# Differential attention in front of a mixture of experts: scores in three single PSUM banks, transposes in two, a later place for each projected tile's transposes, and the output norm spread over the last turns

## The chip, the core and the metric

The kernel runs on one core of a Trainium2 chip. The metric is the device time of one execution in microseconds (us). Of the kernel before there are three runs, from 1671.71 to 1674.43, median 1672.71, and one more execution that was recorded by the hardware profiler.

## The reference, cut to what matters

Two layers work on 256 latent and 256 context tokens of width 1024. Layer 0 is a short gated convolution and a dense SwiGLU. Layer 1, in which the change lies, is differential attention and a mixture of experts. Its attention has 16 heads of 64 in 8 pairs; only the latent tokens ask, and all 512 tokens answer:

```python
def diff_core(q, k, v, lam):
    logits = einsum('bqhd,bkhd->bhqk', q, k) * (HEAD_DIM ** -0.5)
    p = softmax(logits, axis=-1).reshape(b_, h2 // 2, 2, nq, nk)
    w = p[:, :, 0] - lam * p[:, :, 1]
    return einsum('bhqk,bkhe->bqhe', w, v)          # one value of 128 for each pair

q_l, k_l, v_l = proj(a_lat)     # rms_norm of q and k in each head, then rope_2d
q_c, k_c, v_c = proj(a_ctx)     # rms_norm alone
o = rms_norm(o, sub_g) * (1 - lam_init)             # the output norm, over each 128
h = h + g1 * (o.reshape(..., -1) @ w_out)
...
xs = a_pad[slot_tok]            # top 2 of 8 experts for each token
ys = (silu(xs @ w1) * (xs @ w3)) @ w2               # 2816 hidden
```

## The kernel before, in words

**Products.** A large product is three matmuls in a reduced float type (`mm3`, lines 173 to 176): weight and activation are each split in a high and a low part, and high by high, high by low and low by high are added in PSUM. Weights come from HBM in units of 128x2048 float32 (1 MB), 300 and more of them, one after the other on SP's queue (`loads`). `Parts.pump` (line 72) takes a unit that has landed when a slot is free, writes its high part with a cast (ACT, line 80; DVE, line 78, for the units listed in `HV`, here 0 and 63), and subtracts on DVE for the low part (line 84). Its instructions stand in ACT's and DVE's queues at the place where the program calls `pump`, which is inside `parts.unit` (take the next unit), `release` and `give` (line 119: hand back n spent units and prepare one more).

**Order.** The program has a schedule by hand: each engine executes its instructions in the order in which the Python code issues them. The order around the change is therefore made by calls, and by generators that are advanced a few steps at a time.

**Projections.** Four passes, each for two pairs of heads, project queries, keys and values. A pass gives tiles of 128 tokens by 512 columns: A and B (latent queries and keys), D (context keys), C and E (values). `normed` (line 714) takes A, B and D: ACT squares the tile, DVE multiplies by the rope factors and sums the squares, `seed` (704) makes a first guess of the inverse root on DVE, `newton` (706) refines it in eight small POOL instructions, DVE multiplies (743) and PE transposes the tile in four 128x128 pieces (749) that ACT copies to `qk`. Between these come `yield`s, five behind the Newton steps and three behind the multiplication, and at each PE gets another few products of a projection in between (for one step of `projections`, line 765, three matmuls of 512 columns with A and B, six of 256 with C, D and E).

**Turns.** Sixteen turns, one for each pair of a head and 128 queries, and two more to drain (line 929). Turn m issues, in this order: `turn(m-2)`, PE's four transposes of the weights (843) and ACT's copy `wT` (845); `scores(m)`, two matmuls of 512 columns (815); `top(m)`, the row maxima on DVE (819); `weigh(m-1)`, the difference of the two softmaxes on DVE (836 to 838); `soft(m)`, two exponentials on ACT (828); five steps of `fill`, the projections of passes 1 to 3; the output steps; and `value(m-2)` (851). From turn 11 on no projections are left. There the output norm is worked in: `subnorm` (the inverse root), `scaled` (873), `sub_t` (878 transposes; 879 the high part `onh` on ACT; 880 the low part `onl` on DVE) and `outp`, the output projection, whose weights are units 61 to 64.

**PSUM.** Eight banks. In the turns the pool `pss` has two tiles of two banks each for scores, `psw` one bank for transposes (`wt`), `pso` one for values and `psf` two for projections.

**What follows.** `gated` adds to the residual, the routing ranks the experts, and a gather by one-hot matmuls (1130) brings the tokens of an expert together: its result is evicted by DVE (1134), cast by ACT (1136) and subtracted by DVE (1124). Eight experts of 11 chunks each follow: `up`, the gate (Silu on ACT, 1168, and a product on DVE, 1169), two transposes (1175) and `down`. Units 67 and 68 are the weights of the first chunks.

Of the kernel before, what the change touches and what calls it, by code (L numbers as in the profile page):

```python
# [11 lines left out]
F32 = mybir.dt.float32  # L12
# [8 lines left out]
P = 128  # L21
# [9 lines left out]
GROUPS = (6, 8, 8)  # L31
ADA_PE = (0, 1, 3)
NE = 8
HV = (0, 63)
NCH = FT // 2
LAM = 0.8 - 0.6 * math.exp(-0.3)

# [93 lines left out]
def backbone(ctx: ExitStack, tc: tile.TileContext, i, out):  # L131
# [582 lines left out]
    def normed(n, kind, ps, new):  # L714

        sq = pq.tile([P, T2], F32, name="qsq", bufs=2)
        A.activation(sq, ps, AF.Square)
        x = pq.tile([P, T2], F32, name="qx", bufs=3)
        if kind == "D":
            V.tensor_tensor(out=heads(x), in0=heads(ps), in1=qkg[:, None, 64:].to_broadcast([P, 8, 64]), op=OP.mult)  # L720
        else:
            t = "AB".index(kind)
            z = pq.tile([P, T2], F32, name="qz")
            for a in range(2):
                xs = ps[:, half(a)].rearrange("p (h r b j) -> p h r b j", h=4, r=2, b=2)
# [12 lines left out]
        newton(r, m, e)  # L738
        if kind != "D":
            V.tensor_tensor(out=x, in0=x, in1=z, op=OP.add)  # L740
        for _ in range(5):
            yield
        V.tensor_tensor(out=heads(x), in0=heads(x), in1=r[:, :, None].to_broadcast([P, 8, 64]), op=OP.mult)
        for _ in range(3):
            yield
        pt = new()
        for j in range(4):
            c = j % 2 * 2 + j // 2 if kind == "D" else j
            PE.transpose(pt[:, j * P:(j + 1) * P], x[:, c * P:(c + 1) * P], ident)
        if kind == "D":  # L750
            A.copy(qk[n % 2][:, 2:, T:], pt.rearrange("p (j t) -> p j t", j=2))
        else:
            A.copy(qk[n % 2][:, :, t * P:(t + 1) * P], pt.rearrange("p (j t) -> p j t", j=4))
# [42 lines left out]
    loads.advance()  # L796
    l0.close()

    pss = att.enter_context(tc.tile_pool(name="pss", bufs=2, space=PSUM, reuse_waits="tile"))
    psw = att.enter_context(tc.tile_pool(name="psw", bufs=1, space=PSUM, reuse_waits="tile"))  # L800
    pso = att.enter_context(tc.tile_pool(name="pso", bufs=1, space=PSUM, reuse_waits="tile"))
    psf = att.enter_context(tc.tile_pool(name="psf", bufs=2, space=PSUM, reuse_waits="tile"))
    aw = att.enter_context(tc.tile_pool(name="aw", bufs=1, side="right", reuse_waits="tile"))
# [5 lines left out]
    def scores(m):  # L809
        h, t = heads16[m]  # L810
        n, j = h // 2 % 2, h % 2
        ps = S[m] = pss.tile([P, 2, T2], F32, name="sc")
        for a in range(2):
            r = slice(64 * a, 64 * a + 64)
            PE.matmul(ps[:, a], qk[n][r, j, t * P:(t + 1) * P], qk[n][r, 2 + j], start=True, stop=True)

    def top(m):
        mx = sm.tile([P, 2], F32, name="mx")
        V.tensor_reduce(mx, S[m], axis=AX.X, op=OP.max)
        V.tensor_scalar(mx, mx, -0.125, None, op0=OP.mult)  # L820
        return mx

    def soft(m, mx):
        h, t = heads16[m]
        e = E[m] = aw.tile([P, 2, T2], F32, name="e", bufs=3)
        z1 = sm.tile([P, 1], F32, name="z1")
        for a in range(2):
            A.activation(e[:, a], S[m][:, a], AF.Exp, bias=mx[:, a:a + 1], scale=0.125,
                         accum_out=z1 if a else z0[:, t, h:h + 1])
        return z1  # L830

# [91 lines left out]
    def pull(n):  # L923
        for _ in range(n):
            next(fill, None)
# [3 lines left out]
    for m in range(18):  # L929
        if m > 1:  # L930
            turn(m - 2)
        if m < 16:
            scores(m)
            mx = top(m)
        if 0 <= m - 1 < 16:
            weigh(m - 1, zs.pop(m - 1))
        if m < 16:
            zs[m] = soft(m, mx)
        pull(5)
        if m == 13:  # L940
            subnorm(0, 4, 6)
            outp(ops, LO, (0, 1))
        if m == 14:
            subnorm(1, 4, 6)
            outp(ops, LO, (2, 3))
        if m == 15:
            out1 = pss.tile([P, 2, T2], F32, name="sc")
            ops += [out1[:, a, half(b)] for a in range(2) for b in range(2)]
            outp(ops, HI, (0, 1))
        if m == 16:  # L950
            outp(ops, HI, (2, 3))
        if m == 17:
            scaled(0, 6, 8)
            outp(ops, LO, (4, 5))
        if m > 1:
            value(m - 2)
        pull(5 if m < 11 else 99)
        if m == 10:
            for t in range(2):
                subnorm(t, 0, 4)  # L960
        if m == 11:
            for t in range(2):
                scaled(t, 0, 4)
            proj.close()
            held.close()
            pm = more.enter_context(tc.tile_pool(name="more", bufs=1, reuse_waits="tile"))
            parts.free.extend(part_slots(pm, 1, "x"))
            parts.last_use, xlo = parts.free[-1]
            parts.holding = True
            nh, nl = ([pm.tile([P, D], F32R, name=n), parts.last_use[:, c * D:(c + 1) * D]] for c, n in enumerate(("nh", "nl")))  # L970
            small = routing(pm)
            oh = [pm.tile([P, 2, P], F32R, name=f"oh{t}") for t in range(2)]
            po = att.enter_context(tc.tile_pool(name="on", bufs=1, reuse_waits="tile"))
            onh, onl = (po.tile([P, 8, 2, P], F32R, name=f"on{n}") for n in range(2))
            wo = [parts.unit() for _ in range(2)]
            ops = [psf.tile([P, T2], F32, name="mm") for _ in range(2)]
            ops = [ops[a][:, half(b)] for a in range(2) for b in range(2)]
        if m == 12:
            sub_t(0, 0, 4)
            sub_t(1, 0, 4)  # L980
            parts.pump(1)
        if m == 13:
            wo += [parts.unit() for _ in range(2)]
        if m == 14:
            scaled(0, 4, 6)
            sub_t(0, 4, 6)
        if m == 15:
            scaled(1, 4, 6)
            sub_t(1, 4, 6)
        if m == 16:  # L990
            subnorm(0, 6, 8)
            parts.give(1)

        loads.free.extend({11: ada_slots[:1], 15: ada_slots[1:], 17: later[:1]}.get(m, []))
        loads.advance()
    subnorm(1, 6, 8)
    sub_t(0, 6, 8)
    scaled(1, 6, 8)
    outp(ops, HI, (4, 5))
    sub_t(1, 6, 8)  # L1000
    parts.give(1)

    r = small

# [10 lines left out]
    def route_n():  # L1015

        V.tensor_tensor(out=r["ms"], in0=r["ms2"][:, :, 0], in1=r["ms2"][:, :, 1], op=OP.add)
        A.activation(r["ms"], r["ms"], AF.Sqrt, bias=eps, scale=1.0 / D)
        V.reciprocal(r["ms"], r["ms"])

    def route_h(t, n):

# [41 lines left out]
    for k in range(0, KT, 2):  # L1064
        outp(ops, [k, k + 1], (6, 7))
        for n in range(k, k + 2):
            gated(ops[n], n, mod1[8 + k // 2], 0)
        if k == 4:
            both = pss.tile([P, 2, T2], F32, name="sc")
            token_major(0, 0, both[:, 0])  # L1070
            token_major(1, 0, psw.tile([P, T2], F32, name="wt"))
            logits(0)
    token_major(0, 1, both[:, 1])
    token_major(1, 1, psf.tile([P, T2], F32, name="mm"))
    logits(1)
    route_n()
# [9 lines left out]
        onehot(t, 0, 0)  # L1086
    for t in range(2):
        route_l(t, 1)
    for _ in range(2):
        parts.give(1)  # L1090
    att.close()
    fin = ExitStack()
    px = fin.enter_context(tc.tile_pool(name="px", bufs=1, side="right", reuse_waits="tile"))
# [22 lines left out]
    def gather():  # L1116
# [9 lines left out]
        for k in range(KT):  # L1126
# [4 lines left out]
                              start=t == b == 0, stop=t == b == 1)  # L1131
            x = px.tile([P, 2, P], F32, name="gx", bufs=2)
            m = mod1[12 + k]
            V.tensor_scalar(x, ps.rearrange("p (n s) -> p n s", n=2), m[:, 1, 0:1], m[:, 0, 0:1], op0=OP.mult, op1=OP.add)
            for n in range(2):
                A.copy(xs[n][0][:, k], x[:, n])
            if late is not None:
# [88 lines left out]
    for e in range(NE):  # L1226
        for c in range(NCH):
# [11 lines left out]
                        res = None  # L1239
            if e == c == 0:  # L1240
                next(run)
                parts.holding = False
            if e == 0 and c == 1:
                gates()
# [140 lines left out]
```

## Time and profile before

| | us |
|---|---|
| median of three runs | 1672.71 (1671.71 to 1674.43) |
| profiled execution, its own time | 1673.41 |
| its span in the trace | 1671.6 |
| PE busy | 1592.0 (95%) |
| weight loads of PE (beside matmuls) | 1305.6 (78%) |
| DVE busy | 1323.9 (79%) |
| ACT busy | 878.3 (53%) |
| POOL busy | 42.3 (3%) |
| DMA | 400 MB, 239 GB/s over the span |

The profiled execution took 1.8 us more than its span: that part lies around the program and not in it. The stages are found by their lines: layer 0 up to about 605 us, the projections' first pass to 657, turns with projections to 774.5, the last turns to 832, routing and gather to about 864, experts to 1640, then the end. PE is TensorE, DVE VectorE, ACT ScalarE, POOL GpSimd; "PEld" are PE's weight loads, which run beside its matmuls. A share of the whole span says little here, since the stages have different limits; a stage is read by its own window. A name in front of an arrow is what an instruction writes, the names behind it what it reads.

### The profile page before, as it was taken

Reading aid. Unit: us, or ns where it says so; the run is one execution under the profiler, and the core shown is the slowest. Engines: PE = TensorE matmul, PEld = TensorE weight load, DVE = VectorE, ACT = ScalarE, POOL = GpSimd, SP = SyncE. Lnnn points to the kernel's source line nnn. Section 1 sums busy time; section 2 is a strip of 40 time slices with the busy share of each in tenths; the row PEclk is TensorE's granted clock in tenths of the full one; section 3 lists DMA queues with packets and bytes.
Section 4 is the critical chain, followed back from the end, with each engine's and each line's share of the span. In section 5 each row is a group of like instructions: output and inputs, shape, how many; then the busy total and the mean of one; then the engine's idle time right before and its main releaser. Section 6 shows DMA issues by size and latency. Waiting matters only on the chain. (4 is left out here: it accounts for less than half of the span.)

```text
span 1671.6 us, 21025 instructions
## 1 busy us (share of the span) xinstructions
PE 1592.0 (95%) x7767; PEld 1305.6 (78%) x7767; DVE 1323.9 (79%) x1899; ACT 878.3 (53%) x1223; POOL 42.3 (3%) x157
## 2 busy tenths in 40 slices
PE   8799899999999998897889999999999999999997
PEld 7587688888888887776768887788778887788886
DVE  5888887668568574566478898989989898998986
ACT  3222244222222242444457767777667776777774
POOL 0000000000000002112000000000000000000000
PEclk9999999999999998999989999999999999999999
DMA  9345534445547323222249988999889998899990
GB/s 356 110 175 193 188 118 155 152 157 195 176 177 299 129 76 127 76 76 101 102 170 367 364 318 338 349 352 358 317 338 355 353 350 325 328 366 351 357 356 29
DMA packets 55729, 400.36 MB, mean 239 GB/s; under 512 B 6450, under 2 KB 6482, under 8 KB 7106
## 3 DMA queue, kind: packets, MB, share of 16 engines
q1 hardware_dynamic: 55298, 398.50, 63.5%
q8 instruction: 63, 1.03, 0.2%
q0 software_dynamic: 320, 0.44, 0.2%
q14 instruction: 48, 0.39, 0.1%
HBM read 397.87 MB, written 1.05 MB: 239 GB/s over the span
## 5 line engine op out<-in xcount | busy, mean ns | idle before, releaser
L84 DVE TENSOR_TENSOR wl<-rw,wh 128x1024 fp32r<-128x1024 f32 (+1 forms) x220 | 329.2, 1528 | 84.3 <-ACT wh L80 83.7
L80 ACT CAST wh<-rw 128x1024 fp32r<-128x1024 f32 (+1 forms) x219 | 276.3, 1295 | 61.4 <-PE mm L175 56.4
L174 PE MATMUL mm<-ah,wh 128*128 128x512 f32 (+1 forms) x576 | 221.1, 384 | 9.0 <-ACT ah L314 8.1
L176 PE MATMUL mm<-ah,wl 128*128 128x512 f32 (+1 forms) x576 | 220.3, 382 | 5.1 <-DVE wl L84 5.0
L175 PE MATMUL mm<-al,wh 128*128 128x512 f32 (+1 forms) x576 | 220.0, 382 | 0.1
L84 DVE TENSOR_TENSOR wl<-rp,wh 128x1024 fp32r<-128x1024 f32 (+1 forms) x160 | 192.7, 1244 | 21.3 <-ACT wh L80 20.7
L254 DVE SCALAR_TENSOR_TENSOR junk<-ra,cb 128x1024 bf16<-128x1024 f32 x136 | 166.3, 1223 | 3.3
L80 ACT CAST wh<-rp 128x1024 fp32r<-128x1024 f32 (+1 forms) x159 | 162.9, 1065 | 4.4 <-PE y L176 3.1
L176 PE MATMUL y<-wh,hl 128*128 128x512 f32 x352 | 141.4, 402 | 3.9 <-DVE hl L1179 3.9
L174 PE MATMUL h<-wh,xl 128*128 128x512 f32 x352 | 143.6, 408 | 0.0
L174 PE MATMUL h<-wh,xs 128*128 128x512 f32 x352 | 142.8, 406 | 0.0
L175 PE MATMUL h<-wl,xl 128*128 128x512 f32 x352 | 139.9, 397 | 0.0
L174 PE MATMUL y<-wh,hh 128*128 128x512 f32 x352 | 138.9, 395 | 0.5 <-ACT hh L1178 0.5
L175 PE MATMUL h<-wl,xs 128*128 128x512 f32 x352 | 139.2, 395 | 0.0
L175 PE MATMUL y<-wl,hh 128*128 128x512 f32 x352 | 139.0, 395 | 0.0
L176 PE MATMUL h<-wh,xl 128*128 128x512 f32 x352 | 139.0, 395 | 0.0
L176 PE MATMUL h<-wh,xs 128*128 128x512 f32 x352 | 138.9, 395 | 0.0
L174 PEld LDWEIGHTS mm<-ah,wh 128*128 128x128 f32 x576 | 109.9, 191 | 31.2 <-ACT ah L314 9.8
L176 PEld LDWEIGHTS mm<-ah,wl 128*128 128x128 f32 x576 | 109.7, 190 | 27.6 <-DVE wl L84 7.2
L84 DVE TENSOR_TENSOR wl<-ra,wh 128x1024 fp32r<-128x1024 f32 x104 | 122.4, 1217 | 11.1 <-ACT wh L80 9.2
L84 DVE TENSOR_TENSOR wl<-rq,wh 128x1024 fp32r<-128x1024 f32 x104 | 121.9, 1217 | 10.8 <-ACT wh L80 10.2
L175 PEld LDWEIGHTS mm<-al,wh 128*128 128x128 f32 x576 | 110.0, 191 | 21.6 <-DVE al L309 1.2
(286 smaller groups left out, 2926.2 us busy)
## 6 DMA issues: line engine op xcount, KB each, us to landing
rw<-moe SPq DMA_DIRECT2D x81, 1024.0 KB, 5.4
rp<-moe SPq DMA_DIRECT2D x79, 1024.0 KB, 5.2
rw<-w SPq DMA_DIRECT2D x61, 1024.0 KB, 4.8
ra<-moe SPq DMA_DIRECT2D x52, 1024.0 KB, 5.0
rq<-moe SPq DMA_DIRECT2D x52, 1024.0 KB, 5.3
ra<-ada SPq DMA_DIRECT2D x44, 1024.0 KB, 4.9
rx<-ada SPq DMA_DIRECT2D x4, 1024.0 KB, 19.7
rp<-w SPq DMA_DIRECT2D x4, 1024.0 KB, 6.5
```

The lines of the kernel that those rows point to most:

```text
L80: self.nc.scalar.copy(hi[:, c0], raw[:, c0])
L84: engine.tensor_tensor(out=lo[:, c], in0=raw[:, c], in1=hi[:, c].bitcast(F32), op=OP.subtract)
L174: PE.matmul(ps, wh, xh, start=first, stop=False)
L175: PE.matmul(ps, wh, xl, start=False, stop=False)
L176: PE.matmul(ps, wl, xh, start=False, stop=last)
L254: V.scalar_tensor_tensor(junk, raw[:, a * D:(a + 1) * D], 1.0, cb[:, s], op0=OP.mult, op1=OP.mult, accum_out=m[:, a, s:s + 1])
```

## The change

1. `HV` loses unit 63: its cast goes from DVE (78) to ACT (80).
2. In `normed` six steps, not three, stand between the multiplication and the transposes.
3. `pss` has three tiles of one bank for scores, not two of two banks, so a turn takes two tiles; `psw` has two tiles, not one. `top` takes the maxima in two reductions of 512.
4. The output norm is spread: `subnorm` and `scaled` stand ahead of a turn's `pull`, `sub_t` one or two turns earlier. The output projection of the upper four row blocks goes by (4, 5) and then (6, 7) with heads 0 to 3 each, where it went over all four row blocks with heads 0, 1 and then 2, 3.
5. Units are prepared at other places: `parts.give` in turn 17 and within the last output projection; units 67 and 68 behind the gather's last step and not in front of the gather.
6. Behind the root of the routing ACT executes one Silu on a spare value. Every second eviction of the gather goes to ACT.

```diff
-HV = (0, 63)
+HV = (0,)
@@ normed
-        for _ in range(3):
+        for _ in range(6):
             yield
         pt = new()
@@ pools
-    pss = att.enter_context(tc.tile_pool(name="pss", bufs=2, space=PSUM, reuse_waits="tile"))
-    psw = att.enter_context(tc.tile_pool(name="psw", bufs=1, space=PSUM, reuse_waits="tile"))
+    pss = att.enter_context(tc.tile_pool(name="pss", bufs=3, space=PSUM, reuse_waits="tile"))
+    psw = att.enter_context(tc.tile_pool(name="psw", bufs=2, space=PSUM, reuse_waits="tile"))
@@ scores, top
-        ps = S[m] = pss.tile([P, 2, T2], F32, name="sc")
+        ps = S[m] = [pss.tile([P, T2], F32, name="sc") for a in range(2)]
-        V.tensor_reduce(mx, S[m], axis=AX.X, op=OP.max)
+        for a in range(2):
+            V.tensor_reduce(mx[:, a:a + 1], S[m][a], axis=AX.X, op=OP.max)
@@ turns
             zs[m] = soft(m, mx)
+        for t, h0, h1, first in ((0, 0, 4, 10), (1, 0, 4, 10), (0, 4, 6, 12), (1, 4, 6, 14), (0, 6, 8, 16)):
+            if m == first:
+                subnorm(t, h0, h1)
+            if m == first + 1:
+                scaled(t, h0, h1)
+        if m == 17:
+            parts.give(1)
         pull(5)
...
         if m == 15:
-            out1 = pss.tile([P, 2, T2], F32, name="sc")
-            ops += [out1[:, a, half(b)] for a in range(2) for b in range(2)]
-            outp(ops, HI, (0, 1))
+            ops += [ps[:, half(b)] for ps in [pss.tile([P, T2], F32, name="sc") for a in range(2)] for b in range(2)]
+            outp(ops, (4, 5), range(4))
         if m == 16:
-            outp(ops, HI, (2, 3))
+            outp(ops, (6, 7), range(4))
...
@@ turn 11
+            sub_t(0, 0, 4)
         if m == 12:
-            sub_t(0, 0, 4)
             sub_t(1, 0, 4)
             parts.pump(1)
         if m == 13:
+            sub_t(0, 4, 6)
+            parts.pump(1)
             wo += [parts.unit() for _ in range(2)]
-        if m == 14:
-            scaled(0, 4, 6)
-            sub_t(0, 4, 6)
         if m == 15:
-            scaled(1, 4, 6)
             sub_t(1, 4, 6)
-        if m == 16:
-            subnorm(0, 6, 8)
-            parts.give(1)
+        if m == 17:
+            sub_t(0, 6, 8)
...
     subnorm(1, 6, 8)
-    sub_t(0, 6, 8)
+    outp(ops, HI, (4, 5))
     scaled(1, 6, 8)
-    outp(ops, HI, (4, 5))
     sub_t(1, 6, 8)
-    parts.give(1)
@@ route_n
+        A.activation(r["rank"][:, 0, :1], eps, AF.Silu)
@@ last output projection, k = 0, 2, 4, 6
+        if k == 2:
+            parts.give(1)
@@ in front of the gather
-    for _ in range(2):
-        parts.give(1)
@@ gather
+            if k % 2:
+                A.activation(x, ps.rearrange("p (n s) -> p n s", n=2), AF.Identity, bias=m[:, 0, 0:1], scale=m[:, 1, 0:1])
+            else:
                 V.tensor_scalar(...)
@@ first chunk of the first expert
                 next(run)
+                for _ in range(2):
+                    parts.give(1)
```

**How it moves instructions.** PE in the second pass, beside the first turns: `mm` are products of the projection, `sc` the scores, L749 the transposes of a projected tile, L843 (L844 in the changed kernel) those of a turn. Before:

```order
L815 MATMUL sc<-ra_69 128x512 x2
...
L175 MATMUL mm<-wl_77,ah_267 128x256
L176 MATMUL mm<-wh_76,al_275 128x256
L749 MATMUL wt<-ident,qx 128x128 x4
...
L176 MATMUL mm<-wh_74,al_275 128x256
L749 MATMUL wt<-ident,qx 128x128 x4
L843 MATMUL wt<-ident,e 128x128 x4
L815 MATMUL sc<-ra_69 128x512 x2
```

And in the changed kernel:

```order
L815 MATMUL sc<-ra_69 128x512 x2
...
L176 MATMUL mm<-wh_76,al_273 128x256
L749 MATMUL wt<-ident,qx 128x128 x4
...
L176 MATMUL mm<-wh_74,al_275 128x256
L844 MATMUL wt<-ident,e 128x128 x4
L815 MATMUL sc<-ra_69 128x512 x2
...
L176 MATMUL mm<-wh_74,al_273 128x256
L749 MATMUL wt<-ident,qx 128x128 x4
```

The first tile's transposes stand 18 matmuls later behind the scores; the second tile's stood ahead of the next turn's transposes and scores, and now stand 18 matmuls behind them. The pass's third tile, whose L749 stood 12 matmuls ahead of the turn after, now comes 6 matmuls behind that turn's scores.

ACT in turns 10 and 11, the end of the projections: `e` are the exponentials, `wT` a turn's copy, `wh_74` the high part of unit 63 (DVE's in the kernel before, so it isn't in this queue there), `rp_4395` the values' copy, `oo` a turn's output. Before:

```order
L751 COPY ra_70<-wt 128x2x256
L845 COPY wT<-wt 128x512
L828 ACTIVATE e,z_4683<-sc,mx 128x512
L828 ACTIVATE e,z_5879<-sc,mx 128x512
L757 COPY rp_4395<-mm 128x512
L853 ACTIVATE ojunk,ss<-o 128x128
L854 COPY oo_4401<-o 128x128
L845 COPY wT<-wt 128x512
```

And in the changed kernel:

```order
L846 COPY wT<-wt 128x512
L829 ACTIVATE e,z_4683<-sc,mx 128x512
L829 ACTIVATE e,z_5897<-sc,mx 128x512
L751 COPY ra_70<-wt 128x2x256
L80 CAST wh_74<-rp_4396 128x2048
L757 COPY rp_4395<-mm 128x512
L854 ACTIVATE ojunk,ss<-o 128x128
L855 COPY oo_4401<-o 128x128
L880 ACTIVATE on_5980<-wt,subg 128x4x128
L846 COPY wT<-wt 128x512
```

The copy of the last projected tile moved behind the exponentials, the cast of unit 63 stands behind it, and the high part of the first output norm ahead of the next turn's `wT`.

ACT from the gather to the first gate: `xl` and `xs` are casts of gathered tokens, `wh_74` and `wh_76` the high parts of units 67 and 68, `ga` the Silu of a chunk. Before:

```order
L1023 ACTIVATE xh_5925<-mm,ms 128x512
L80 CAST wh_74<-rw_71 128x2048
L1136 CAST xl_5926<-gx 128x128
...
L1136 CAST xs_6504<-gx 128x128
L80 CAST wh_76<-rp_4396 128x2048
L1168 ACT_TABLE_LOAD
L1168 ACTIVATE ga<-h_6537 128x256
```

And in the changed kernel:

```order
L1016 ACT_TABLE_LOAD
L1016 ACTIVATE rank<-eps 128x1
L1020 ACTIVATE nh<-sc,ms 128x512
...
L1131 ACTIVATE gx<-g,mod_19_3696 128x256
L1135 CAST xl_5950<-gx 128x128
L1135 CAST xs_6536<-gx 128x128
L80 CAST wh_74<-rw_71 128x2048
L80 CAST wh_76<-rp_4396 128x2048
L1167 ACTIVATE ga<-h_6569 128x256
```

Both casts now stand in one piece between the last gathered tile and the first gate, and the table load of the Silu stands ahead of the gather.

## Rows read from the trace of the kernel before

**Rows 1.** windows by stage: length, busy (count) of PE, PEld, DVE, ACT, POOL; clock; DMA

```profile
620.00:774.50 154.50, 137.26 (x890) 117.36 (x888) 90.35 (x171) 64.71 (x127) 28.40 (x104) 0.96 0.24 86
774.50:832.00 57.50, 43.55 (x304) 36.17 (x304) 30.46 (x63) 23.84 (x61) 8.16 (x38) 0.91 0.31 111
832.00:870.00 38.00, 29.88 (x174) 25.85 (x175) 26.55 (x59) 19.83 (x39) 0.00 (x0) 0.82 0.39 150
870.00:1640.00 770.00, 766.07 (x3476) 615.28 (x3475) 699.38 (x846) 571.79 (x747) 0.00 (x0) 1.00 0.89 342
```

**Rows 2.** waits of PE from 600 to 880 us: line, releaser, total, times, longest

```profile
PE wt L749 <- DVE qx L743: 12.0, 7, 3.5
PE wt L878 <- DVE on L880: 4.6, 1, 4.6
PE wt L843 <- DVE on L880: 4.3, 3, 1.6
PE mm L749 <- DVE qx L743: 3.2, 1, 3.2
PE g L1130 <- DVE gx L1134: 2.2, 1, 2.2
PE wt L843 <- ACT ra L753: 2.0, 3, 0.7
PE wt L749 <- DVE sq L862: 1.6, 1, 1.6
```

**Rows 3.** windows: 256-column matmuls at full clock, and two stretches at half clock

```profile
619.00:625.00 6.00, 6.00 (x52) 6.00 (x52) 6.00 (x18) 3.76 (x8) 0.00 (x0) 1.00 0.37 152
649.30:656.13 6.83, 5.72 (x16) 4.56 (x16) 2.89 (x2) 0.59 (x1) 0.20 (x1) 0.50 0.71 259
789.25:799.49 10.24, 5.65 (x19) 3.42 (x20) 5.76 (x7) 5.24 (x11) 0.00 (x0) 0.50 0.47 167
```

**Rows 4.** timeline, turns with projections: start, duration, instruction, count, idle time before it

```profile
668.31 0.63 PE L749 MATMUL wt<-ident,qx 128*128 128x128 f32 x4 [1.07 <-DVE qx L743]
...
677.54 0.63 PE L749 MATMUL wt<-ident,qx 128*128 128x128 f32 x4 [2.68 <-DVE qx L743]
...
679.43 1.13 PE L815 MATMUL sc<-ra 64*128 64x512 f32 x4
...
682.62 0.69 ACT L828 ACTIVATE e<-sc,mx 128x512 f32<-128x512 f32 x1 [2.50 <-DVE zr L836]
...
688.93 0.63 PE L749 MATMUL wt<-ident,qx 128*128 128x128 f32 x4 [1.55 <-DVE qx L743]
```

**Rows 5.** timeline of DVE and POOL about 645 us

```profile
645.21 2.29 DVE L84 TENSOR_TENSOR wl<-rw,wh 128x2048 fp32r<-128x2048 f32 x1
645.39 2.17 POOL L709 TENSOR_TENSOR qe<-qr 128x8 f32<-128x8 f32 x1 [9.65 <-DVE qr L704]
```

**Rows 6.** timeline of DVE in the last turns

```profile
782.71 1.31 DVE L78 CAST wh<-rp 128x2048 fp32r<-128x2048 f32 x1 [0.52 <-PE mm L176]
...
787.47 1.22 DVE L819 TENSOR_REDUCE mx<-sc 128x2 f32<-128x1024 f32 x1
...
789.24 0.75 DVE L838 SCALAR_TENSOR_TENSOR e<-e,zr 128x512 f32<-128x512 f32 x1
```

**Rows 7.** timeline from the gather to the second MoE chunk

```profile
851.87 2.28 DVE L84 TENSOR_TENSOR wl<-rw,wh 128x2048 fp32r<-128x2048 f32 x1
...
862.87 1.90 ACT L80 CAST wh<-rp 128x2048 fp32r<-128x2048 f32 x1
...
864.79 1.28 ACT L1168 ACT_TABLE_LOAD   x1
...
866.09 0.39 ACT L1168 ACTIVATE ga<-h 128x256 f32<-128x256 f32 x1
...
867.02 0.42 DVE L1169 TENSOR_TENSOR ga<-h,ga 128x256 f32<-128x256 f32 x1
...
867.49 0.44 PE L1175 MATMUL ht<-ident,ga 128*128 128x128 f32 x2 [1.44 <-DVE ga L1169]
```

More of the change, by code (lines that the diff above doesn't have):

```diff
@@ L811, in scores @@
         n, j = h // 2 % 2, h % 2
-        ps = S[m] = pss.tile([P, 2, T2], F32, name="sc")
+        ps = S[m] = [pss.tile([P, T2], F32, name="sc") for a in range(2)]
         for a in range(2):
             r = slice(64 * a, 64 * a + 64)
-            PE.matmul(ps[:, a], qk[n][r, j, t * P:(t + 1) * P], qk[n][r, 2 + j], start=True, stop=True)
+            PE.matmul(ps[a], qk[n][r, j, t * P:(t + 1) * P], qk[n][r, 2 + j], start=True, stop=True)
     def top(m):
         mx = sm.tile([P, 2], F32, name="mx")
-        V.tensor_reduce(mx, S[m], axis=AX.X, op=OP.max)
+        for a in range(2):
+            V.tensor_reduce(mx[:, a:a + 1], S[m][a], axis=AX.X, op=OP.max)
         V.tensor_scalar(mx, mx, -0.125, None, op0=OP.mult)
@@ L827, in soft @@
         for a in range(2):
-            A.activation(e[:, a], S[m][:, a], AF.Exp, bias=mx[:, a:a + 1], scale=0.125,
+            A.activation(e[:, a], S[m][a], AF.Exp, bias=mx[:, a:a + 1], scale=0.125,
                          accum_out=z1 if a else z0[:, t, h:h + 1])
@@ L938, in backbone @@
             zs[m] = soft(m, mx)
+        for t, h0, h1, first in ((0, 0, 4, 10), (1, 0, 4, 10), (0, 4, 6, 12), (1, 4, 6, 14), (0, 6, 8, 16)):
[5 more added lines that the diff above has]
+            parts.give(1)
         pull(5)
         if m == 13:
-            subnorm(0, 4, 6)
             outp(ops, LO, (0, 1))
         if m == 14:
-            subnorm(1, 4, 6)
             outp(ops, LO, (2, 3))
         if m == 15:
-            out1 = pss.tile([P, 2, T2], F32, name="sc")
-            ops += [out1[:, a, half(b)] for a in range(2) for b in range(2)]
-            outp(ops, HI, (0, 1))
+            ops += [ps[:, half(b)] for ps in [pss.tile([P, T2], F32, name="sc") for a in range(2)] for b in range(2)]
+            outp(ops, (4, 5), range(4))
         if m == 16:
-            outp(ops, HI, (2, 3))
+            outp(ops, (6, 7), range(4))
         if m == 17:
-            scaled(0, 6, 8)
             outp(ops, LO, (4, 5))
@@ L957, in backbone @@
         pull(5 if m < 11 else 99)
-        if m == 10:
-            for t in range(2):
-                subnorm(t, 0, 4)
         if m == 11:
-            for t in range(2):
-                scaled(t, 0, 4)
             proj.close()
@@ L1067, in backbone @@
             gated(ops[n], n, mod1[8 + k // 2], 0)
+        if k == 2:
+            parts.give(1)
         if k == 4:
-            both = pss.tile([P, 2, T2], F32, name="sc")
-            token_major(0, 0, both[:, 0])
+            token_major(0, 0, pss.tile([P, T2], F32, name="sc"))
             token_major(1, 0, psw.tile([P, T2], F32, name="wt"))
             logits(0)
-    token_major(0, 1, both[:, 1])
+    token_major(0, 1, psw.tile([P, T2], F32, name="wt"))
     token_major(1, 1, psf.tile([P, T2], F32, name="mm"))
@@ L1133, in gather @@
             m = mod1[12 + k]
-            V.tensor_scalar(x, ps.rearrange("p (n s) -> p n s", n=2), m[:, 1, 0:1], m[:, 0, 0:1], op0=OP.mult, op1=OP.add)
+            if k % 2:
+                A.activation(x, ps.rearrange("p (n s) -> p n s", n=2), AF.Identity, bias=m[:, 0, 0:1], scale=m[:, 1, 0:1])
+            else:
+                V.tensor_scalar(x, ps.rearrange("p (n s) -> p n s", n=2), m[:, 1, 0:1], m[:, 0, 0:1], op0=OP.mult, op1=OP.add)
             for n in range(2):
```

## The prediction

> **What bounds the kernel now.** The table of windows by stage comes first [rows 1]. From 870 to 1640 us, the experts, PE is busy 766.07 of 770 us, with DVE at 699 and DMA at 0.89: nothing that the change does can make that stretch shorter, and it can only be held up by PE itself. The attention that stands in front of it is different: PE idles 17.2 of 154.5 us while the turns still have projections beside them (620 to 774.5), 13.95 of 57.5 us in the last turns (774.5 to 832), and 8.1 of 38 us from there to the second chunk of the first expert. So the time of this kernel is PE's work in order, plus these 39 us, plus what the half clock costs. Second view: PE's waits in that stretch [rows 2]. Nearly all the idle time before 774.5 is at L749, the transposes of a projected tile, which wait for the multiply of L743 on DVE (12.0 and 3.2 us), and at L843, where a turn's transposes wait for a bank of `psw` that ACT's copy still reads (2.0). In the last turns it is L878 and L843, held by the single `psw` bank until L880 has read it (4.6 and 4.3). Third: the clock. Two stretches at a granted clock of 0.50, which is the 1.2 GHz level, follow on the long idle times: 649.30 to 656.13, behind the 3.5 us wait, and 789.25 to 799.49, in the wait of 4.6 [rows 3]. PE was busy 5.72 and 5.65 us in them, work that takes about half as long at the upper level: 2.9 and 2.8 us lost.
>
> **First pass, 620 to 657.** The first tile's transposes move behind 18 matmuls of 256 columns, the third tile's behind 9 of 512. 52 of the former fill 6 us [rows 3], 0.12 each, and I take twice that for 512 columns. The chains on DVE and POOL in front of L743 don't change, so of 3.2 us 3.2 - 2.2 = 1.0 stay and of 3.5 us 3.5 - 2.05 = 1.45 [rows 2]. One wait is new: the first scores now stand 3 matmuls, not 12, behind the last transposes, and ACT's copy of those lies between; 0.5 us (bounds 0 and 1.1). With a wait of 1.45 I expect no half clock behind it, which gives back 2.9. Term 1: 6.7 - 2.95 + 2.9 = 6.6 us; without the clock 3.7, and 9 if the earlier low stretches go too.
> Why 1.45 stays: POOL's first Newton step took 2.17 us there and ended as DVE's subtraction of 2.29 us ended, where its later steps are short [rows 5]. That subtraction still stands between the seed and L743. The Trainium skill, "SBUF — State Buffer", Who interferes with whom, says that a VectorE instruction with two SBUF inputs holds the read port that GpSimd needs for its whole length; the trace agrees with 2.17 beside 2.29. Had POOL run through, nothing of the 1.45 would be left and the term would be 8.0.
>
> **Turns with projections, 657 to 774.5.** What is left there is 12.0 - 3.5 + 2.0 = 10.5 us [rows 2]. The L843 waits go with the second `psw` bank. The tiles' waits were 2.68 at most [rows 4], and each L749 now stands at least 18 matmuls later (2.2 us), the second and third tile of a pass behind a turn's transposes and scores as well (0.6 and 1.1). But the chain doesn't get shorter. In the second pass the third tile's multiply is behind a weight subtraction, that behind a cast on ACT, and that behind the exponentials of 682.62 [rows 4]; PE came to it at 688.93 - 1.55 = 687.4. It now comes 1.07 + 2.68 + 0.7 = 4.4 us earlier by the waits that are gone and 3.9 later by the move: it waits about 2.0, and the second tile's transposes 0.5. In the later passes less was waited ahead of it, so the move covers all. Term 2: 10.5 - 2.5 = 8.0 us; bounds 5.5 (the same return in all passes) and 10.5.
> The reduction in two halves costs nothing here: 1.22 us [rows 6] becomes at most two times 0.7, and DVE is busy 90 of 154.5 us [rows 1].
>
> **Last turns, 774.5 to 832.** To be won: 13.95 us idle and 2.8 of clock, 16.7. Four waits come in, all from the queues' order. (a) Unit 63's cast leaves DVE, where it took 1.31 [rows 6], for ACT, where such a cast takes 1.90 [rows 7]; it stands ahead of turn 10's copy `wT`, so `value(10)` waits about 1.6. (b) On DVE the subtraction of unit 63 (2.28, as in [rows 7]) and the first normed tile's low part (0.75) come before turn 12's maxima (1.4) and `weigh(11)` (0.75 and two small ones, 1.2 in all); turn 11's transposes wait about 1.9. (c) The first output projection waits for the second normed tile's low part: 0.8. (d) `sub_t(0, 4, 6)` waits for `scaled`, which is now behind unit 64's subtraction (2.28), a maximum and a `weigh`, while PE has only 24 matmuls and a `value` to do: 2.7. Sum 7.0, and 0.4 more where the last `sub_t` is followed at once by the output projection. I take 2.5 us for half clock, since the four fall within 15 us, and nothing for the third bank of scores (below). Term 3: 16.7 - 7.4 - 2.6 = 6.7 us. Bounds 1 (each of the four a little longer than the wait that it replaces) and 13 (ACT and DVE come through early).
>
> **Routing and gather.** In front of the gather DVE did unit 67's subtraction, 2.28 us, while PE waited 2.2 for the first eviction [rows 2, 7]. That preparation moves behind the gather; the eviction then waits for the one-hot and low parts only, and I keep 0.7 of the 2.2. The Silu table is loaded behind the root instead: 1.28 us [rows 7] ahead of ACT's four evictions, most of it beside DVE's ranking, 0.3 us. Term 4: 1.5 - 0.3 = 1.2; bounds -1 and 3.
> The Trainium skill, "ScalarE: Activation LUTs", What ACT_TABLE_LOAD costs, gives about 1.28 us for the load and 1.38 for a drain, 2.66 for a switch. In this trace the activation starts 0.02 us behind a load of 1.28 [rows 7], so the drain isn't there. By the page the term would be -0.2 and the time 1655.
>
> **First chunks of the first expert.** This is the part that costs. Both casts of units 67 and 68 now stand on ACT between the gather's last copies and the Silu of the first chunk, both subtractions on DVE ahead of the product. The gather's last copy ended at 862.87; PE waited 1.44 at 867.49 with six matmuls of the second chunk done, so it had ended the first chunk at about 867.49 - 1.44 - 1.4 = 864.65, 1.8 later [rows 7]. Counted from the last copy: unit 67 ready at 1.90 + 2.28 = 4.2, PE there at 1.8, wait 2.4; six matmuls to 5.6; product at 4.2 + 2.28 + 0.42 = 6.9, wait 1.3. Sum 3.7 against 1.44, and 0.7 for a stretch at half clock: term 5 is -3.0. Bounds -1 (the cast starts early) and -5.5. It happens once: in the experts DVE needs 699 of 770 us and catches up.
>
> **Sum.** 6.6 + 8.0 + 6.7 + 1.2 - 3.0 = 19.5 us. The profiled execution took 1673.41 us with a span of 1671.6; 1673.4 - 19.5 = 1653.9. It lies 0.7 above the median of the three runs, 1672.71, which is less than my terms are good for. I say 1654.
>
> **Rivals.**
> 1. The chains set the pace. If DVE, ACT and POOL lie on the path in every pass, term 2 falls to 3, term 3 to 2: 6.6 + 3 + 2 + 1.2 - 3 = 9.8, 1664 us. For it: the order of DVE's queue, and the wait that I found in the second pass. Against it: DVE is busy 58% and ACT 42% there [rows 1].
> 2. The last turns come out clean: term 3 at 13, terms 2 and 5 at 9 and -1: 6.6 + 9 + 13 + 1.2 - 1 = 28.8, 1645 us. For it: (a) to (d) rest on ACT and DVE being no earlier than in the trace, and PE's earlier arrival moves some of their inputs up.
> 3. Slower: the three-bank rotation. A turn's second score matmul now needs the bank of the turn before's first half, which is free when its first exponential has ended. In turn 2 that was from 679.43 to 682.62 + 0.69, 3.9 us [rows 4]; PE is back after 60 matmuls of 0.12 and three small steps, over 9 us. It decides only where the way from scores to exponential gets longer than the turn; to end 0.2% slower it must cost 19.5 + 3.4 = 23 us over 15 turns, so some 11 us instead of 3.9: 1677 us.
> 4. Nothing moves: the waits only change their places, within 3 us of 1673. It needs every term at its lower bound (3.7 + 5.5 + 1 - 1 - 5.5 = 3.7).
>
> **How the numbers follow.** Forecast 0.62, rival 1 0.16, rival 2 0.14, rival 3 0.04, rival 4 0.04. About 0.2% is what a measurement of this kernel can tell from no change. The range takes in the forecast with its bounds and most of rivals 1 and 2: 1643 to 1665. Faster 0.92, same 0.04, slower 0.04.
>
> **What would show it.** Term 1: no half clock after the third tile's L749, and an idle time of 1 to 1.5 there. Term 2: none of PE's waits on L749 in the third and fourth pass, one of about 2 us in the second. Term 3: PE waiting at the output of turn 10 for `wT`, at turn 11's transposes, and at `sub_t(0, 4, 6)`. Term 5: PE waiting over 2 us for unit 67's low part in the second chunk. The prediction is wrong if PE waits at the scores (rival 3), if L749 still waits in every pass (rival 1), or if the last turns have no wait over 1 us (rival 2).

## The result

The changed kernel takes 1633.73 us (median of four runs, 1632.38 to 1634.29) against 1673.57 for the kernel before: 0.9761 of its time, 95% interval 0.9744 to 0.9778. That is 39.8 us less, where 19.5 were forecast; the time lies below the range. The profiled execution took 1633.3 us with a span of 1631.5.

The page of the changed kernel, first row; columns: busy time, share, instructions:

```profile
PE 1584.1 (97%) x7767; PEld 1307.2 (80%) x7767; DVE 1317.6 (81%) x1898; ACT 890.2 (55%) x1241; POOL 44.5 (3%) x157
```

PE executes as many instructions as before and is busy 8 us less, so by the view 32 of the 40 us were idle time. To see where they went, both traces are cut at the same instructions: the scores of turns 1 and 10, the last `sub_t`, the last step of the first gather, and the first and last `down`. The cuts lie up to 8 us off the borders of the forecast's stretches, but up to the last turns PE has no wait in between in the kernel before. The kernel before, windows; columns as in [rows 1]:

```profile
0.00:664.48 664.48, 631.02 (x3042) 527.06 (x3042) 482.52 (x784) 201.97 (x257) 15.98 (x47) 0.98 0.49 175
664.48:766.55 102.07, 91.53 (x614) 77.09 (x613) 61.54 (x116) 44.75 (x95) 16.05 (x64) 1.00 0.18 62
766.55:831.25 64.70, 51.11 (x363) 43.01 (x363) 35.98 (x73) 28.25 (x70) 10.28 (x46) 0.92 0.31 111
831.25:861.21 29.96, 22.91 (x143) 20.37 (x142) 19.50 (x48) 12.25 (x28) 0.00 (x0) 0.77 0.40 154
861.21:872.13 10.92, 9.48 (x46) 7.32 (x44) 8.71 (x23) 9.52 (x14) 0.00 (x0) 1.00 0.53 204
872.13:1659.14 787.01, 782.61 (x3549) 628.33 (x3548) 710.95 (x850) 580.77 (x759) 0.00 (x0) 1.00 0.87 334
```

The changed kernel, the same stretches:

```profile
0.00:654.43 654.43, 630.57 (x3042) 527.26 (x3042) 483.78 (x787) 202.20 (x257) 16.92 (x49) 0.98 0.49 177
654.43:745.42 90.99, 89.46 (x610) 76.66 (x609) 58.82 (x121) 43.53 (x94) 14.92 (x62) 1.00 0.22 76
745.42:799.16 53.74, 49.37 (x368) 42.61 (x367) 37.45 (x79) 29.79 (x72) 12.67 (x46) 0.97 0.34 120
799.16:825.89 26.73, 21.68 (x144) 19.63 (x142) 16.06 (x44) 13.43 (x32) 0.00 (x0) 0.81 0.48 193
825.89:841.44 15.55, 12.59 (x45) 8.98 (x44) 12.08 (x24) 12.19 (x16) 0.00 (x0) 0.78 0.55 199
841.44:1618.90 777.46, 777.00 (x3549) 629.62 (x3548) 704.69 (x837) 588.31 (x770) 0.00 (x0) 1.00 0.88 337
```

Microseconds gained in each stretch:

| stretch | forecast | measured |
|---|---|---|
| first pass (term 1) | 6.6 | 10.05 |
| turns with projections (term 2) | 8.0 | 11.1 |
| last turns (term 3) | 6.7 | 11.0 |
| routing, gather (term 4) | 1.2 | 3.2 |
| first chunks (term 5) | -3.0 | -4.6 |
| experts | 0 | 9.55 |
| sum | 19.5 | 40.2 |

The waits that are left on PE between 600 and 880 us, the changed kernel; columns: line, releaser, total, times, longest:

```profile
PE o L1048 <- DVE sel L1042: 2.1, 1, 2.1
PE wt L844 <- DVE e L839: 1.9, 1, 1.9
PE h L175 <- DVE wl L84: 1.8, 1, 1.8
PE g L1126 <- DVE oh L1057: 1.8, 1, 1.8
PE wt L749 <- DVE qx L743: 1.5, 1, 1.5
...
PE o L852 <- ACT wT L846: 1.3, 1, 1.3
PE wt L879 <- DVE oo L874: 1.2, 1, 1.2
PE mm L749 <- DVE qx L743: 1.0, 1, 1.0
PE ht L1174 <- DVE ga L1168: 0.9, 1, 0.9
```

Of the 15.2 us at L749 and the 8.9 behind L880 [rows 2], 2.5 and nothing are left.

### The profile page after: what moved, and what is told of

It is laid out like the page before. It is cut to its first block, busy times and chain, and to the rows that moved or that the text cites. A ratio compares the mean times of both kernels' runs of the same rounds, so it can differ in the third digit from the quotient of the medians.

```text
span 1631.5 us, 20995 instructions
## 1 busy us (share of the span) xinstructions
PE 1584.1 (97%) x7767; PEld 1307.2 (80%) x7767; DVE 1317.6 (81%) x1898; ACT 890.2 (55%) x1241; POOL 44.5 (3%) x157
## 5 line engine op out<-in xcount | busy, mean ns | idle before, releaser
L175 PE MATMUL mm<-al,wh 128*128 128x512 f32 (+1 forms) x576 | 221.5, 384 | 0.0
L175 PE MATMUL h<-wl,xl 128*128 128x512 f32 x352 | 140.9, 400 | 1.8 <-DVE wl L84 1.8
L175 PE MATMUL y<-wl,hh 128*128 128x512 f32 x352 | 139.1, 395 | 0.0
L175 PE MATMUL h<-wl,xs 128*128 128x512 f32 x352 | 139.0, 395 | 0.0
L175 PEld LDWEIGHTS mm<-al,wh 128*128 128x128 f32 x576 | 110.8, 192 | 21.5 <-DVE al L309 0.9
```

Of the source, the lines that this page charges most:

```text
L175: PE.matmul(ps, wh, xl, start=False, stop=False)
```

## The experiments

All times are medians; the kernel before took 1673.6 to 1675.0 in these comparisons. Each run begins from one of the two kernels and makes the edit that is shown or named. A letter (theory A) is that of the run's own expectation.

**The gather's evictions.** The largest miss is in the experts, where the forecast saw no gain. PE's only waits between 870 and 1640 us in the kernel before are these:

```profile
PE y L176 <- DVE hl L1179: 3.9, 21, 0.2
```

e1, the kernel before with this edit alone:

```diff
+            if k % 2:
+                A.activation(x, ps..., AF.Identity, bias=m[:, 0, 0:1], scale=m[:, 1, 0:1])
+            else:
                 V.tensor_scalar(x, ps..., m[:, 1, 0:1], m[:, 0, 0:1], ...)
```

> The kernel before with one edit: every second eviction of the gather on ACT. Theory (the gather's way through DVE and ACT sets the pace of the chunks that hold a gather step): the 21 waits of PE for the low part hl between 870 and 1640 us go. Each is shown as 0.18 us, but the starts of the two matmuls there lie 0.57 and 0.34 us apart where 0.235 is usual, so each costs 0.44: 21 x 0.44 = 9.2 us, and up to 1 more in the first gather. 1663 to 1665 us. Rival 1 (as the forecast had it, the eviction counts only in the first gather): 1672 to 1674. Rival 2 (only the chunks whose own eviction moved gain, about half of the 21): 1668 to 1670.

Measured: 1664.5 us, 0.9952 (0.9938 to 0.9966), 9.2 us less, and no wait of PE is left between 870 and 1640. Between the same instructions of `down` the experts take 9.55 us less than before, so this edit alone gives all that they gained. e2, the changed kernel without it (all of the gather's evictions on DVE):

> The changed kernel with all of the gather's evictions back on DVE. Theory of the gather's loop: the stalls come back, 21 of them at 0.44 us, and the time is 1633.7 + 9.2 = 1643, up to 1644 with the first gather. Rival (the units' new places, not the eviction, took these stalls away): under 1636.

Measured: 1640.5 us, 6.8 more. Its waits of PE from 600 to 1640 us show the stalls again, all 21:

```profile
PE y L176 <- DVE hl L1175: 4.0, 21, 0.2
```

Between the same instructions of `down`, the experts took 9.6 us longer than in the changed kernel; the other 2.6 us it was ahead when the first `down` began, 1.1 of it already at the first scores. So the theory stands, with its size (the time came out 2.5 under the 1643 expected, by those 2.6). How one stall looks, kernel before, PE, a chunk with a gather step:

```profile
1016.22 0.40 PE L174 MATMUL y<-wh,hh 128*128 128x512 f32 x1
1016.46 0.40 PE L175 MATMUL y<-wl,hh 128*128 128x512 f32 x1
1017.03 0.50 PE L176 MATMUL y<-wh,hl 128*128 128x512 f32 x1 [0.18 <-DVE hl L1179]
1017.37 0.40 PE L174 MATMUL y<-wh,hh 128*128 128x512 f32 x1
```

The view shows 0.18 us idle. But these matmuls start 0.235 us apart when nothing waits (their records of 0.40 overlap); here it is 0.57 and 0.34. The loss is 0.335 + 0.105 = 0.44, and 21 of them are 9.2. Between the starts of two gather steps a chunk that stalls takes 9.53 us (1000.39 to 1009.92), one of the changed kernel 9.08 (987.43 to 996.51): 0.455 more, 21 times, are the 9.55 measured. Why `hl` is late, same chunk, ACT:

```profile
1012.80 0.30 ACT L1136 CAST xl<-gx 128x128 fp32r<-128x128 f32 x1 [2.80 <-DVE gx L1134]
...
1013.21 1.99 ACT L80 CAST wh<-rq 128x1024 fp32r<-128x1024 f32 x2
```

And DVE:

```profile
1012.23 0.54 DVE L1134 TENSOR_SCALAR gx<-g,mod 128x256 f32<-128x256 f32 x1
...
1014.28 2.36 DVE L84 TENSOR_TENSOR wl<-rq,wh 128x1024 fp32r<-128x1024 f32 x2 [1.11 <-ACT wh L80]
1016.56 0.42 DVE L1179 TENSOR_TENSOR hl<-ht,hh 128x256 fp32r<-128x256 f32 x1
```

DVE and ACT wait for each other in a circle. ACT idles 2.80 us for DVE's eviction, which stands behind a weight subtraction; the next weight's cast stands on ACT behind the gather's casts, so DVE idles 1.11 for it; and `hl` stands behind that subtraction. No engine of the two is full (DVE busy 8.44 of 9.55 us, ACT 6.75), yet the circle is longer than PE's chunk of 9.08. In the changed kernel an eviction on ACT breaks it, ACT in a chunk with one:

```profile
960.87 0.56 ACT L1131 ACTIVATE gx<-g,mod 128x256 f32<-128x256 f32 x1 [0.62 <-PE g L1126]
961.46 0.30 ACT L1135 CAST xl<-gx 128x128 fp32r<-128x128 f32 x1
...
961.87 2.00 ACT L80 CAST wh<-ra 128x1024 fp32r<-128x1024 f32 x2
```

And DVE:

```profile
962.94 2.36 DVE L84 TENSOR_TENSOR wl<-ra,wh 128x1024 fp32r<-128x1024 f32 x2
965.22 0.42 DVE L1178 TENSOR_TENSOR hl<-ht,hh 128x256 fp32r<-128x256 f32 x1
```

DVE's subtraction now follows with no idle time: DVE is busy 9.09 of the 9.09 us of this chunk. Half of the gather's chunks keep their eviction on DVE, and they don't stall either. e7 asks why, with `k % 4 == 3` in place of `k % 2`:

> The changed kernel with two of eight gather evictions on ACT (the fourth and the eighth), not four. It tells how the stalls went from the chunks whose own eviction stayed on DVE. Theory A (each chunk for itself, so all four had to be moved and the others had slack anyway): the stalls of the chunks that went back return, about 10 to 11 of 21, at 0.44: 1638 to 1639. Theory B (a chunk with its eviction on ACT lets DVE catch up, and the chunk behind lives on that): with one in four, two or three chunks of every four stall, 10 to 15 stalls: 1638 to 1640, and the stalls stand in the chunks farthest behind one on ACT, none in the one directly behind. Theory C (one in four is enough): 1633 to 1635. What tells A from B is which chunks stall.

Measured: 1637.4 us, 3.6 more. Six stalls, in no chunk but the second and third of each gather:

```profile
PE y L176 <- DVE hl L1178: 1.1, 6, 0.2
```

The fourth, on ACT, is followed by three on DVE without a stall that the view shows. No theory had the count right; A, each chunk for itself, is wrong, and B, a chunk that lives on the one ahead, has the cause. The trace of e7 shows a lead that is used up. Behind an eviction on ACT, DVE's own come 1.16, 1.61 and 2.07 us behind the start of their chunk's gather, 0.45 later each time, which is what the circle (9.53) is longer than PE's chunk (9.08). The next one would lie beyond the 2.3 us that the stalled chunks show (1009.92 to 1012.23 in the kernel before). The third chunk already takes 9.30 us, so it loses 0.22 with no idle time in the view. So one eviction on ACT serves its own chunk and two more wholly, the third in part; the changed kernel, with one in two, never gets beyond 1.16 behind one on ACT.

**Six steps, and three.** e3, the kernel before with `range(6)` in `normed` and nothing else:

> The kernel before with six steps, not three, in front of the projected tiles' transposes; one bank for transposes as before. Theory A (each removed wait gives back what is shown and about 0.26 us more, because a matmul's record ends after the next could have started; nothing of the chains shows behind the move): the waits at L749, 12.0 + 3.2 us in 8, go but for some 1, so 14 + 2, and 2.9 of half clock: 1655 to 1658. Theory B (the forecast's: the chains on DVE and ACT hold part back): 6.6 in the first pass and 5.5 behind it, about 12: 1661 to 1663. Theory C (the single bank then makes the copies of these transposes collide with the turns' own, and L843 waits instead): gain under 8, above 1666.

Measured: 1653.1 us, 0.9887 (0.9870 to 0.9904), 20.6 less: by the medians more than theory A said, though the interval (16 to 22 us) reaches into its range, and half of the whole change by one number. Theories B and C fall. Of the 15.2 us at L749 1.0 is left (L843 waits 1.7 for ACT's copies), and the windows of this run show no half clock from 620 to 762 us, where the kernel before had three stretches of it (629, 636 and 649 us, 13.7 us in all; of the other kernels with six steps all but e2 had one stretch of 3.4 or 6.8 at about 631):

```profile
620.00:657.00 37.00, 35.96 (x244) 31.40 (x243) 24.86 (x50) 15.34 (x22) 14.34 (x40) 1.00 0.44 159
657.00:762.00 105.00, 102.11 (x708) 87.96 (x707) 71.20 (x136) 51.56 (x112) 19.43 (x74) 1.00 0.24 81
```

e5, the changed kernel with `range(3)`:

> The changed kernel with three steps, not six, in front of the projected tiles' transposes. Theory A (the move is what took the waits at L749 away, and the copies of the tiles on ACT then hold up the squares and casts behind them): it loses what the move alone gave, 20.6, less the 2 to 3 us that the second transposes' bank saves there anyway: 1651 to 1654, with L749 waiting 12 to 15 us. Theory B (two banks for transposes already take most of these waits): under 1645.

Measured: 1658.0 us, 24.3 more, with 16.8 us of waits at L749: theory A, and larger than its 1651 to 1654, so the second transposes' bank takes nothing from these waits (16.8 us in the kernel before too, with the 1.6 behind L862 [rows 2]). e13 parts PE's transposes from ACT's copy of them:

```diff
             PE.transpose(pt[:, j * P:(j + 1) * P], x[:, c * P:(c + 1) * P], ident)
+        for _ in range(3):
+            yield
         if kind == "D":
             A.copy(...)
```

> The changed kernel with three steps in front of PE's transposes of a projected tile, as before, but ACT's copy of them three steps later, so that the copy stands on ACT where six steps put it and only PE's part stands where three put it. The kernel with both at three took 1658.0 and waited 16.8 us at L749. Theory A (part of those waits came from ACT's own queue: the copy waits there for PE and holds up the squares and casts that the next tiles' chains need, so the chains got shorter with the move): L749 waits 8 to 13 us and the time is 1650 to 1655. Theory B (the chains are as long either way, and six steps only put more work in front of PE): L749 waits 16 to 17 us and the time is 1656 to 1659.

Measured: 1654.4 us, 3.6 less than e5, with 15.8 us at L749: between the two theories. The intervals of the two runs (0.9874 to 0.9918 and 0.9865 to 0.9898) overlap, so the time settles little; the timeline of PE does. e5, third tile of the first pass and of the third pass:

```profile
651.06 1.08 PE L749 MATMUL wt<-ident,qx 128*128 128x128 f32 x4 [3.35 <-DVE qx L743]
...
732.12 0.99 PE L749 MATMUL wt<-ident,qx 128*128 128x128 f32 x4 [2.50 <-DVE qx L743]
```

And e13:

```profile
648.33 0.63 PE L749 MATMUL wt<-ident,qx 128*128 128x128 f32 x4 [0.79 <-DVE qx L743]
...
728.20 0.68 PE L749 MATMUL wt<-ident,qx 128*128 128x128 f32 x4 [2.50 <-DVE qx L743]
```

In the first pass the wait falls by 2.56 us, and the stretch at half clock behind it is gone; in the third and fourth pass all waits stay (in the second pass one grew, from 0.92 to 2.51, where e5 had run at half clock). So in the first pass ACT's copy, which waits there for PE, did hold up the chain of the next tile. The kernel before, ACT:

```profile
638.99 0.59 ACT L753 COPY ra<-mm 128x512 f32<-128x512 f32 x1 [3.34 <-PE mm L749]
639.47 1.91 ACT L80 CAST wh<-rw 128x2048 fp32r<-128x2048 f32 x1
641.28 0.59 ACT L717 ACTIVATE qsq<-mm 128x512 f32<-128x512 f32 x1
```

ACT idles 3.34 us at the copy, and the cast and the square that DVE needs next stand behind it. In e13 the cast comes ahead of the copy:

```profile
637.31 1.90 ACT L80 CAST wh<-rw 128x2048 fp32r<-128x2048 f32 x1 [1.04 <-PE mm L176]
640.48 0.60 ACT L717 ACTIVATE qsq<-mm 128x512 f32<-128x512 f32 x1 [1.27 <-PE mm L176]
640.97 0.58 ACT L755 COPY ra<-mm 128x512 f32<-128x512 f32 x1
```

**The banks.** e4, the kernel before with the new banks and the maxima in halves, order as before:

> The kernel before with three single banks for scores, two for transposes and the maxima in two halves; order as before. Theory A (the waits that the one bank causes are real): L843 behind ACT's copies, 2.0 us in 3, and L878 and L843 behind L880, 4.6 and 4.3, go, with 0.26 us more for each and up to 2.8 of half clock: gain 8 to 13, 1660 to 1666. Theory B (the low part of the output norm and the weights come as late as before, so the wait moves to the output projection): gain 2 to 5, 1668 to 1672. Rival (three banks for scores hold the turns up): slower than 1674, with PE waiting at the scores.

Measured: 1669.9 us, 0.9981 (0.9971 to 0.9991), 3.8 less: theory B. Waits of PE from 774 to 840 us:

```profile
PE wt L844 <- DVE on L881: 4.0, 1, 4.0
...
PE sc L174 <- ACT e L829: 0.8, 1, 0.8
```

Two `sub_t` in a row take both banks, so the turn's transposes behind them wait for L881 as they did for L880. PE never waited at the scores. The three banks cost one wait, 0.8 us, where the first output projection takes a score bank and waits for an exponential; the changed kernel doesn't have it.

**What the rest is worth.** e6, the kernel before with six steps, the banks and the gather's evictions:

> The kernel before with three parts of the change: six steps, the new banks, and every second eviction of the gather on ACT. The output norm, the places where units are prepared, unit 63's cast and the Silu stay as before. Theory A (the parts add up): 1673.7 - 20.6 - 3.8 - 9.2 = 1640; what is left to the changed kernel, 6 us, is the spread output norm (about 10) less the later units (about 4). Theory B (the second bank's gain is partly the same wait that the move removes): 1641 to 1643. Rival (the spread norm is worth nothing): 1634.

Measured: 1638.9 us. The parts add up (33.6 us by themselves, 34.7 to 35.7 together), and 5.1 is left for the spread norm and the moved units. Cut at the same instructions, the changed kernel gains 6.4 over e6 in the last turns (the wait of 4.0 at L844 stands in e6 too), 2.4 in routing and gather, and loses 4.6 in the first chunks. No run has the spread norm by itself; the 6.4 is a difference between two kernels that also differ in unit 63's cast, which e10 below shows to be worth nothing there.

**The later units.** e9 puts units 67 and 68 back in front of the gather; e8 prepares 67 inside it:

```diff
                 if e == c == 0:
                     next(run)
+                    if k == 0:
+                        parts.give(1)
...
-                for _ in range(2):
-                    parts.give(1)
+                parts.give(1)
```

> The changed kernel with units 67 and 68 prepared in front of the gather, as in the kernel before. Theory A (the later place gains some 2.4 us in the gather and loses some 4.7 in the first chunks, as the run with three parts of the change shows beside the changed kernel): 1630.5 to 1632.5, with PE waiting about 2.2 us for the gather's first eviction and 1 to 1.5 in the first chunk. Theory B (only the place of the wait changes): 1633 to 1635.

> The changed kernel with unit 67 prepared inside the gather (behind its fourth step), unit 68 behind its last step as in the changed kernel. Theory A (the first chunk waits only because both casts stand behind the gather's last copies): of the waits of 0.2, 1.8, 1.3 (unit low parts) and 0.9 us in the first chunks, some 3 us with what the records hide go, up to 2 more of half clock behind them, and the cast of 1.9 us costs at most 1 in the gather: 1629 to 1631.5. Theory B (the wait moves into the gather, whose evictions then stand behind cast and subtraction): 1633 to 1635, with PE waiting 2 us at the gather's matmuls.

Measured: e9 1632.6 us, 1.1 less than the changed kernel, which the scatter of single runs (1630.3 to 1634.2) doesn't tell from no difference; e8 1631.1 us, 2.6 less (all five runs below the lowest of the changed kernel, though the intervals of the two ratios overlap). In e9 the gather waits 2.2 us for its eviction again. e8 loses the 1.8 us at L175 and keeps 1.9 in the gather, waits of PE from 600 to 1640 us:

```profile
PE g L1126 <- DVE gx L1133: 1.9, 1, 1.9
```

The waits hardly differ in sum. What does differ in the two traces: e8 has no stretch at half clock behind 823 us, and the changed kernel has one. The changed kernel, window of that stretch (the clock is the third number from the end):

```profile
832.95:839.78 6.83, 5.89 (x17) 4.07 (x16) 5.57 (x15) 3.69 (x6) 0.00 (x0) 0.50 0.96 356
```

And e11, which has the same waits, in the same window:

```profile
832.95:839.78 6.83, 5.73 (x26) 4.21 (x27) 6.37 (x15) 5.99 (x9) 0.00 (x0) 1.00 0.86 303
```

From the gather's last step to the first `down` it is 15.55 us in the changed kernel and 13.1 in e11, so that stretch costs about 2.4.

**Unit 63, the Silu, a seventh step.** e10 sets `HV = (0, 63)` in the changed kernel, e11 leaves the Silu out, e12 is e8 with `range(7)`:

> The changed kernel with unit 63's cast on DVE, as before. Theory A (the cast only trades places: 1.90 us on ACT ahead of turn 10's copy, where PE waits 1.3, against 1.31 on DVE ahead of turn 12's maxima and the difference of turn 11, where PE waits 1.9 already): the first wait goes, the second grows by as much: 1632.5 to 1635. Theory B (DVE is the tighter of the two there): 1635 to 1637.

> The changed kernel without the Silu behind the root of the routing, so that the table is loaded in front of the first gate again. Theory A (1.28 us of loading stand on the path of the first chunk and on none in the routing): 1634.5 to 1636. Theory B (the load also delays ACT's evictions in front of the gather, so it costs as much there as it saves): 1633 to 1634.

> The changed kernel with unit 67 prepared inside the gather (1631.1 so far) and seven steps, not six, in front of the projected tiles' transposes. Theory A (the two waits that are left at L749, 1.0 and 1.5 us, go with what the records hide, 0.26 each, and the first scores, now directly behind the third tile's transposes, wait some 1.2 for ACT's copy): 1629 to 1630.5. Theory B (the copies of the tiles now come too late for the scores or collide with the turns' copies on ACT): 1631 to 1634.

Measured: e10 1633.2 us, as theory A said: the wait for `wT` (1.3) is gone, the one of L844 is 3.1 where it was 1.9. e11 1632.8: no loss, which speaks against its theory A; its waits are those of the changed kernel within 0.2 us, and its profiled execution was without the half clock shown above, so the Silu's place decides nothing that can be seen. e12 1629.9 us, 0.9739 (0.9726 to 0.9752), in theory A's range and 1.2 under e8, which is within the scatter: one wait of 0.8 at L749 is left, and a new one of 0.7 at the first scores, for ACT's copy. It is the lowest median of all, 3.8 below the changed kernel, though the two intervals still overlap.

## Why the prediction was wrong

**The direction and most places were right, the size was half.** Three steps failed. None of the prediction's own signs of being wrong came up (a wait at the scores, L749 waiting in every pass, last turns without a wait over 1 us), and none of them looked at the experts.

1. *"Nothing that the change does can make that stretch shorter."* This was read from a busy share of 766 of 770 us, so the experts stand in the sum at nothing, and they gained 9.55 us. The changed eviction was priced for the first gather alone; the three later gathers stand inside the experts. The 3.9 us that PE did idle there are the 21 waits on `hl` shown under e1. e1 and e2 show that the eviction takes them away. DVE's 699 of 770 us also hid that it spent part of the rest in a circle with ACT.

2. *The waits were priced at the idle time that the view shows.* A matmul's record ends after the next could have started (0.40 us long, 0.235 apart), so what a wait costs is more than its idle time: 0.44 for 0.18 at the stall above. In the turns with projections the idle time fell from 10.54 to 1.53, by 9.0, but the stretch got 11.1 shorter: the other 2.1 us were booked as busy (some 0.35 of them are four transposes that the change moved behind the cut). The residue itself was right in place and nearly in size: 1.5 us at the third tile of the second pass, where 2.0 were forecast, 0.5 at the second, where nothing is.

3. *"The chains on DVE and POOL in front of L743 don't change."* In the first pass they did, by ACT's queue: e13 shows 2.56 us of it. So the 1.45 us that were to stay at the third tile are gone, as are the 0.5 forecast for the first scores, and two of three stretches at half clock went instead of one. PE's waits there fell from 6.7 to 1.0 us, by 5.7 where 3.75 were forecast; the other 4.4 of the 10.05 are clock and what the records hide, where 2.9 were forecast. The first tile's 1.0 came out as forecast (1.02). POOL's long step was forecast right (2.3 us beside a subtraction, in the changed kernel too), but its multiply is done before PE comes.

**Last turns.** The waits were over-priced more than misplaced. Three of the four forecast ones are there: (a) 1.3 for `wT` (1.6 forecast), (b) 1.9 at turn 11's transposes (1.9), (d) 1.2 at `sub_t(0, 4, 6)` (2.7). (c) isn't seen. They add up to 4.4, not 7.4, with one stretch of 3.4 us at half clock where the kernel before has 10.2. (The sum of this term takes 2.6 us for half clock where its text says 2.5, which changes nothing.) By the difference of e6 and the changed kernel the spread norm is worth 6.4 of the 11.0.

**Term 4** was too low in part because PE doesn't wait for the gather's first eviction now (2.2 before, 0.7 forecast to stay). That and the 0.3 that the Silu was to cost, of which no wait shows anything, are 1.0 of the 2.0 us missed; this execution also has 10.2 us at half clock there, where the one before had 13.7, and what that is worth was not measured apart. **Term 5** had its places right (2.0 at unit 67's parts, 2.4 forecast; 0.9 for the product of the gate, 1.3 forecast), but the half clock behind them costs more than the 0.7 that it was given: between 834.7 and 839.4 us matmuls start 0.43 us apart, not 0.235, some 2 us. e11, without that stretch, loses 2.2 us in these chunks, about the 2.3 that the waits were given. The rival of a slower kernel (3) had no support: nothing waits at the scores.

## What to carry to other kernels

Price a wait by the distance between the starts of the instructions around it, not by the idle time shown, and look for a wait that is small but stands in every round of the long loop: 0.18 us, 21 times, was worth 9.55. A busy engine of 99% doesn't prove that its stretch cannot get shorter, and two engines at 88% and 71% can set the pace together when each waits for the other in a circle. Each engine here executes in the order of the code, so a copy that waits holds up all that stands behind it; moved later, it made the chain of the next tile 2.56 us shorter.

## What was not expected of the hardware

One eviction in four on ACT keeps its chunk and the next two at 9.08 us, where all seven chunks behind the first took 9.53 before: a lead of 1.15 us lasts until it is used up, 0.45 a chunk. And the half clock falls differently in executions with nearly the same waits: 832.95 to 839.78 us at 0.50 in the changed kernel, 1.00 in e11, with waits within 0.2 us of each other, and 2.4 us between them. Executions of the kernel before go the same way (1670.74 us at a mean granted clock of 0.986, 1679.94 at 0.977); the four of the changed kernel show no such order. What decides where it falls was not tried.
